# Hybrid decoder layer on one Trainium2 core: heads' keys side by side with zeros for 128-row logits, padded stacks, first transfers on one queue

## The chip, the core and the metric

The kernel runs on one core of one Trainium2 chip. The metric is the device time of one execution in microseconds (us). Times of before are a median of 3 runs; one further execution was profiled. Engines are named as in the profile: PE is the matrix engine, DVE the vector engine, ACT the scalar engine, POOL the GpSimd engine, SP the sync engine (here it only starts transfers). PEld is PE's weight load, which overlaps its matmuls.

## The reference

One decoder layer, with T = 256 positions, width 1024, and four branches of 4 heads by 64, all in fp32:

```python
h = rmsnorm(x, pre_norm_g)
proj = einsum('btd,dc->btc', h, w_in)            # 1024 x 4104
p_gdn, p_hgrn, p_moba, p_diff = split(proj)
y = concat([gdn_branch(p_gdn, ...),              # gated delta rule, chunks of 64
            hgrn2_branch(p_hgrn, ...),           # gated linear recurrence, chunks of 16
            moba_branch(p_moba, slopes_moba),    # one block of 256 keys: causal attention with ALiBi
            diff_branch(p_diff, ...)])           # softmax(q1 k1) - lam * softmax(q2 k2), 32 rows each
y = einsum('btc,cd->btd', y, w_out)              # 1024 x 1024
x = x + rmsnorm(y, post_norm_g)
```

In both attentions the logits of a head are its queries times its keys: 64 deep in MoBA, twice 32 deep in the differential attention. Each branch's output is multiplied by SiLU of its own gate.

## The kernel before

**Arithmetic.** An fp32 product is made of three matmuls. A weight piece (`raw`) is split into a high part in the format fp32r (`whi`, a copy on ACT) and a remainder (`wlo`, a subtraction on DVE); the activations are split likewise into `hT_hi` (ACT) and `hT_lo` (DVE), for 8 slices (k-tiles) of 128 of the 1024 columns. Then hi times hi, hi times lo and lo times hi are summed in PSUM. Small products of the branches (logits, transposes, chunks of the recurrences) are plain fp32.

**Pieces.** `w_in` comes in 32 pieces of two k-tiles each (512 or 520 KB), `w_out` in 8 of 512 KB. In the order of the program: `gkq` (GDN's keys and queries), `gv` (its values and gates), `mqk` (MoBA), `dqk` (differential), `mvz`, `hqf` and `hiz` (HGRN), `dvz`, then `w_out`. Four pieces make one projection. `raw` is a ring of 6 buffers, `whi` and `wlo` rings of 4. So a split waits until PE has used the piece four before it, and a transfer until DVE has split the piece six before it.

**The start.** The transposed `x` (`pxt`) comes in 5 transfers: `h_kd` holds the constants and k-tile 0 (145.5 KB), the four `prob` tiles hold k-tile 1 (128 KB) and k-tiles 2 and 3, 4 and 5, 6 and 7 (256 KB each). ACT's queue starts all five; SP's queue starts the weights. The first weight piece comes and is split in halves, the others whole. PE is kept at work by WARM matmuls on zeros until the first operands are there.

**The order.** Each operation is recorded with its engine, a cost and what it depends on (`record`). `plan` then orders every engine's stream by list scheduling: of the operations that are ready in its model, the one with the greatest rank goes next. The rank is the longest chain of costs behind an operation, plus a boost and a lead for its part of the program (`LEAD`; m and d are the logits of MoBA and differential attention, g GDN, h HGRN, M and D the values of the two attentions, o the output projection). `HOLD` is how much rank ACT gives up to stay with its table of functions, `STAY` how much PE gives up to stay in its tile shape; `LAT` and `free` are what the model holds for hand-offs and for the first moment of an engine. `emit` issues all of it from L392, so nearly every row of the profile has that line, and rows are told apart by their tiles. Engines only run their streams in that order and wait at each instruction for its operands.

**The logits.** PE works in tile shapes (rows by columns): 128 by 128 in the projections, 64 by 128 in MoBA's logits, 64 by 64 in GDN, 96 by 128 in the differential logits. MoBA's keys are `m_k` on the tile `kf`: head 2hp + hh stands in rows 64hh to 64hh + 63 of column block hp. `moba` loops over query blocks j (0 and 1) and over hh, and `softmax_unit` does two 64-row matmuls each, one for each hp. Then come two maxima on DVE (`prob` and `mx`), two exponentials on ACT, a reciprocal on DVE (`m_sum`), two scalings on ACT, and transposes on PE (`probs_t`). In the differential branch `d_st` holds 96 rows of stacked parts (32 by 3), which POOL's transfers (`move`) fill from `d_ks` and `qk4k`.

**HGRN's values.** `vexp` holds each chunk's values in its own 32 rows and zeros elsewhere; it is zeroed once at the start (128 by 2048) and filled late by 4 transfers of SP.

Of the kernel before, what the change touches and what calls it, by code (L numbers as in the profile page):

```python
# [29 lines left out]
D = 1024  # L30
T = 256
# [55 lines left out]
WARM = 18  # L87
# [10 lines left out]
class Core:  # L98
# [5 lines left out]
    HOLD = 71859  # L104
    SWITCH, KEEP, STAY = 95, 1e9, 10357
    LEAD = {'h': 9467, 'g': 7491, 'o': -78342, 'M': -634, 'x': 25587, 'm': 2702, 'd': 2886, 'D': 6239}
    WINDOW = 4096 / 1.2
    LAT = {"PE": 200, "DVE": 170, "ACT": 170, "POOL": 170, "SP": 1900}
# [186 lines left out]
    def plan(self, noise=None):  # L295
# [3 lines left out]
        lat = lambda p, o: 0 if p.eng == o.eng and p.eng == "PE" else (90 if p.eng == o.eng and p.fn != "dma_start" else p.lat)  # L299
# [13 lines left out]
        free = dict(dict.fromkeys(self.engines, 0.0), SP=500.0)  # L313
# [92 lines left out]
def _build(c, x, pxt, w_in, w_out, cst, prow, out, dbg):  # L406
# [14 lines left out]
    XPARTS = [(1, 2), (2, 4), (4, 6), (6, 8)]  # L421
# [20 lines left out]
    def piece(key, k):  # L442

        if (key, k) not in HI:
            t = c.tmp("raw", [128, 2, 520], bufs=6)
            first = not HI
# [3 lines left out]
            c.boost = turn(k) - 0.05 * BOOST if lead < 8 else turn(8) if lead < 10 else 0.0  # L450
            if first:
                c.dma(t[:, 0, :w], part[:, 0])
                c.boost = turn(1) - 0.05 * BOOST
                c.dma(t[:, 1, :w], part[:, 1])
            else:
                c.dma(t[:, :, :w], part)
            split([(key, k), (key, k + 1)], t[:, :, :w], first)
        return HI[key, k], LO[key, k]

    def split(keys, raw, apart=False):  # L460

        w = raw.shape[2]
        c.boost = BOOST
        hi = c.tmp("whi", [128, 2, 520], bufs=4, dt=FR)[:, :, :w]
        lo = c.tmp("wlo", [128, 2, 520], bufs=4, dt=FR)[:, :, :w]
        for i in ([slice(0, 1), slice(1, 2)] if apart else [slice(0, 2)]):
            if apart and i.start == 0:
# [380 lines left out]
    def hgrn_v(pi):  # L848

        vh = c.tile("h_v", [128, 2, 256])  # L850
        for j in range(2):
            act(vh[:, j, :], pi[j], AF.Copy, scale=rs[:, j:j + 1])
        for q in range(4):
            r = slice(32 * q, 32 * q + 32)
            c.dma(vexp[r, :, q, :], vh[r, :, :])
        return vh

    def hgrn(pq, pf, vh):
# [42 lines left out]
        for j in range(2):  # L901
            pu = c.bank("gB" if j == 0 else "gA")
            n = 4 - j
            for hp in range(2):
                for hh in range(2):
                    h = 2 * hp + hh
                    mm(pu[64 * hh:64 * hh + 64, hp * 256:hp * 256 + n * 64], kdh[:, j, h * 64:(h + 1) * 64],
                       vexp[:, j, 0:n, h * 64:(h + 1) * 64])
# [49 lines left out]
    def softmax_unit(bank, lhs, rhs, slope, j, dst, sums):  # L958


        nk = 128 * (j + 1)
        pb = c.bank(bank)
        for hp in range(2):
            mm(pb[:, hp * nk:(hp + 1) * nk], lhs[:, hp, j * 128:(j + 1) * 128], rhs[:, hp, 0:nk])
        mx = c.tmp("mx", [128, 4], bufs=4)
        for hp in range(2):
            c.vec("tensor_tensor_reduce", dst[:, hp, 0:nk],
                  dict(in0=pb[:, hp * nk:(hp + 1) * nk], in1=cs[:, K_DIST + 256 - nk:K_DIST + 256]), scale=1.0,
                  scalar=-3.0e38, op0=OP.add, op1=OP.max, accum_out=mx[:, hp:hp + 1])
        k0 = slope(0)[0]  # L970
        c.tt(mx[:, 2:4], mx[:, 0:2], cs[:, k0:k0 + 3:2], OP.mult)
        for hp in range(2):
            act(dst[:, hp, 0:nk], dst[:, hp, 0:nk], AF.Exp, scale=slope(hp)[1], bias=mx[:, 2 + hp:3 + hp],
                accum_out=sums[:, hp:hp + 1])

    def probs_t(pt, hh, j, P, bank):
        pb = c.bank(bank)
        i = 0
        for hp in range(2):
            for b in range(j + 1):  # L980
                tr(pb[:, i * 128:(i + 1) * 128], P[:, hp, b * 128:(b + 1) * 128], ident)
                i += 1
        o = 2 * j
        act(pt[:, hh, o:o + i].rearrange("p a b -> p (a b)"), pb[:, 0:i * 128], AF.Copy)
# [59 lines left out]
    def diff(pq, pk):  # L1044
# [20 lines left out]
        for hh in range(2):  # L1065
            P = []
            for w in range(2):
# [5 lines left out]
                for j in range(2):  # L1073
                    P.append(c.tmp("prob", [128, 2, 256], bufs=4))
                    softmax_unit("wB", st[0:96, 0], st[0:96, 1],
                                 lambda hp: (K_SL + 4 + 2 * hp + hh, 2.0 ** -(2 * (2 * hp + hh) + 1)), j, P[-1],
                                 sums[:, w, hh, j])
            for j in range(2):
# [7 lines left out]
                probs_t(pt, hh, j, P[j], "wA")  # L1086
# [155 lines left out]
```

## Time and profile before

| | us |
|---|---|
| median of 3 runs | 174.97 (173.48 to 176.22) |
| profiled execution | 175.41 |
| its span in the trace | 173.7 |
| PE busy | 160.8 (93%) |
| PEld busy | 140.1 (81%) |
| DVE busy | 132.9 (77%) |
| ACT busy | 106.8 (61%) |
| POOL busy | 15.7 (9%) |

The span begins and ends inside the execution: 1.7 us of the profiled time lie outside it. A row of a timeline has the start, the length, the engine and the operation with its output and inputs; in brackets stands how long the engine had been idle just before and what ended that. Matmuls are pipelined, so a row's length is longer than its step: the step is read from one start to the next. On PE one fp32 matmul leaves two records, an fp32r matmul one.

### The profile page before, as it was taken

Reading aid. Unit: us, or ns where it says so; the run is one execution under the profiler, and the core shown is the slowest. Engines: PE = TensorE matmul, PEld = TensorE weight load, DVE = VectorE, ACT = ScalarE, POOL = GpSimd, SP = SyncE. Lnnn points to the kernel's source line nnn. Section 1 sums busy time; section 2 is a strip of 40 time slices with the busy share of each in tenths; the row PEclk is TensorE's granted clock in tenths of the full one; section 3 lists DMA queues with packets and bytes.
Section 4 is the critical chain, followed back from the end, with each engine's and each line's share of the span. In section 5 each row is a group of like instructions: output and inputs, shape, how many; then the busy total and the mean of one; then the engine's idle time right before and its main releaser. Section 6 shows DMA issues by size and latency. Waiting matters only on the chain.

```text
span 173.7 us, 3605 instructions
## 1 busy us (share of the span) xinstructions
PE 160.8 (93%) x1358; PEld 140.1 (81%) x1358; DVE 132.9 (77%) x354; ACT 106.8 (61%) x211; POOL 15.7 (9%) x35
## 2 busy tenths in 40 slices
PE   7759999999999999699999997999999999999960
PEld 4559999899997999698788994776877768987850
DVE  0777599695798999994656996976889668759472
ACT  2684757999634264424598928898699631366440
POOL 8000000000000000265007500000000000000000
PEclk9858999999999999999999999999999999999997
DMA  5999897266194037335004899457706100000033
GB/s 164 339 415 418 338 367 261 55 202 199 53 312 157 0 116 235 138 76 110 0 4 91 218 296 398 149 180 246 248 0 189 56 0 0 4 0 0 0 121 121
DMA packets 14176, 27.24 MB, mean 157 GB/s; under 512 B 1360, under 2 KB 2640, under 8 KB 14160
## 3 DMA queue, kind: packets, MB, share of 16 engines
q1 hardware_dynamic: 12288, 24.39, 40.8%
q0 software_dynamic: 1152, 1.57, 4.4%
q10 hardware_dynamic: 720, 1.07, 2.0%
q8 instruction: 10, 0.16, 0.4%
q14 instruction: 6, 0.05, 0.1%
HBM read 24.14 MB, written 1.05 MB: 145 GB/s over the span
## 4 chain that ended last, share of the span: by engine, by line
PE 74%; DVE 12%; DMA 7%; ACT 2%; issue 1%; ACTq 1%; DVEq 0%
PE pj L392 49%; PE gA L392 7%; PE gB L392 7%; PE wB L392 6%; PE wA L392 6%; DVE wlo L392 5%; DMA prob<-in_pxt_dram 4%; DMA raw<-in_w_in_dram 3%; DVE g_nb L392 2%; ACT whi L392 1%; DVE g_vb L392 1%; ACTq L392 1%; DVE g_y L392 1%; DVE b4k L392 1%; DVE lf L392 1%
## 5 line engine op out<-in xcount | busy, mean ns | idle before, releaser
L392 DVE TENSOR_TENSOR wlo<-raw,whi 128x1024 fp32r<-128x1024 f32 (+2 forms) x41 | 48.1, 1197 | 11.1 <-ACT whi L392 6.4
L392 ACT ACTIVATE whi<-raw 128x1024 fp32r<-128x1024 f32 (+2 forms) x40 | 41.4, 1047 | 19.1 <-PE pj L392 12.0
L392 PE MATMUL pj<-hT_hi,whi 128*128 128x256 f32 x144 | 38.8, 293 | 4.1 <-ACT whi L392 1.9
L392 PE MATMUL pj<-hT_lo,whi 128*128 128x256 f32 x144 | 38.1, 290 | 0.0
L392 PEld LDWEIGHTS pj<-hT_hi,whi 128*128 128x128 f32 x144 | 28.1, 196 | 6.0 <-ACT whi L392 3.8
L392 PE MATMUL pj<-hT_hi,wlo 128*128 128x256 f32 x144 | 28.9, 292 | 0.2 <-DVE wlo L392 0.2
L392 PEld LDWEIGHTS pj<-hT_lo,whi 128*128 128x128 f32 x144 | 28.1, 197 | 0.1
L392 PE MATMUL pj<-whi,hT_lo 128*128 128x512 f32 (+2 forms) x80 | 26.7, 348 | 0.0
L392 PEld LDWEIGHTS pj<-hT_hi,wlo 128*128 128x128 f32 x144 | 22.2, 194 | 0.9 <-DVE wlo L392 0.6
L392 PE MATMUL pj<-wlo,hT_hi 128*128 128x512 f32 (+2 forms) x64 | 21.3, 348 | 0.7 <-DVE wlo L392 0.7
L392 PE MATMUL pj<-whi,hT_hi 128*128 128x512 f32 (+2 forms) x64 | 21.4, 342 | 0.5 <-DVE gz_moba L392 0.5
L392 PEld LDWEIGHTS pj<-whi,hT_lo 128*128 128x128 f32 x80 | 15.0, 188 | 1.7
L392 PEld LDWEIGHTS pj<-whi,hT_hi 128*128 128x128 f32 x64 | 12.0, 189 | 2.1 <-DVE gz_moba L392 0.9
L390 ACT ACT_TABLE_LOAD x9 | 11.5, 1283 | 3.4 <-issue 3.2
L392 PEld LDWEIGHTS pj<-wlo,hT_hi 128*128 128x128 f32 x64 | 11.6, 188 | 2.3 <-DVE wlo L392 1.1
L392 ACT ACTIVATE prob<-prob,mx 128x128 f32<-128x128 f32 (+1 forms) x24 | 10.7, 448 | 3.4 <-DVE mx L392 3.3
L392 DVE CUSTOM_DVE_ANT_0 prob<-wB,cs 128x128 f32<-128x128 f32 (+1 forms) x24 | 7.8, 356 | 6.4 <-PE wB L392 6.4
L392 POOL DMA_DIRECT2D d_st<-d_ks x12 | 6.1, 506 | 68.2 <-ACT d_ks L392 68.2
L392 PE MATMUL pj<-whi,d_st 128*128 128x512 f32 (+1 forms) x32 | 10.1, 390 | 0.0
L392 POOL DMA_DIRECT2D d_st<-qk4k x12 | 5.9, 492 | 13.5 <-PE wB L392 11.8
L392 PEld LDWEIGHTS pj<-whi,d_st 128*128 128x128 f32 x32 | 5.4, 189 | 1.1 <-DVE d_st L392 0.2
L392 ACT ACTIVATE t2k<-pj 128x512 f32<-128x512 f32 (+1 forms) x4 | 2.2, 544 | 5.3 <-PE pj L392 5.3
(269 smaller groups left out, 287.4 us busy)
## 6 DMA issues: line engine op xcount, KB each, us to landing
raw<-in_w_in_dram SPq DMA_DIRECT2D x27, 512.0 KB, 5.9
raw<-in_w_out_dram SPq DMA_DIRECT2D x8, 512.0 KB, 4.5
raw<-in_w_in_dram SPq DMA_DIRECT2D x4, 520.0 KB, 8.2
xs<-in_x_dram SPq DMA_DIRECT2D x2, 512.0 KB, 8.5
prob<-in_pxt_dram ACTq DMA_DIRECT2D x3, 256.0 KB, 6.8
d_st<-d_ks POOLq DMA_DIRECT2D x12, 64.0 KB, 2.0
d_st<-qk4k POOLq DMA_DIRECT2D x12, 64.0 KB, 2.0
raw<-in_w_in_dram SPq DMA_DIRECT2D x2, 256.0 KB, 3.7
```

The lines of the kernel that those rows point to most:

```text
L390: nc.scalar.add_instruction(mybir.InstLoadActFuncSet(name=nc.get_next_instruction_name(), act_func_set_id=cur, ins=[], outs=[]))
L392: getattr(self.engines[o.eng], o.fn)(*o.args, **o.kw)
```

## The change

- **MoBA's keys.** `m_k` is now [128, 2, 2, 256]: for each hp and hh a block of 256 columns that holds the keys of head 2hp + hh in their 64 rows and zeros in the other 64. One 128-row matmul gives the logits of both heads of a pair side by side (256 columns for j = 0, 512 for j = 1), where two 64-row ones were. The loop runs over hp where it ran over hh, and the maxima, exponentials and transposes follow. `m_k` stands on the first of two halves of what was `vexp`.
- **Padding.** Rows 96 to 127 of both `d_st` buffers are zeroed once by POOL, and the differential logits read 128 rows.
- **Zeros for HGRN.** `vexp` is split into two tiles. `spread` zeroes both on POOL behind MoBA's logits, and the values come in 8 transfers of 32 KB, not 4 of 64 KB.
- **The start.** The transfers of k-tiles 1 to 7 of `x` go from ACT's queue to SP's, where they stand between the weight pieces in the order of k. The second weight piece is loaded and split in halves too. The copy of the constants `pc` gets the lowest rank in place of the common one.
- **Numbers of the planner**: WARM, HOLD, STAY, LEAD, LAT and `free`.

```diff
-WARM = 18
+WARM = 19
-    HOLD = 71859
-    SWITCH, KEEP, STAY = 95, 1e9, 10357
+    HOLD = 34479
+    SWITCH, KEEP, STAY = 95, 1e9, 8733
...
-    for a, b in XPARTS:
+    for a, b in ((1, 2), (2, 4), (4, 6), (6, 8)):
         c.boost = turn(a)
         c.dma(xr[a // 2][:, a % 2:a % 2 + b - a],
-              pxt[:, P_END + a * T:P_END + b * T].rearrange("p (k t) -> p k t", t=T), "ACT")
+              pxt[:, P_END + a * T:P_END + b * T].rearrange("p (k t) -> p k t", t=T))
...
+            first = lead < 4
             if first:
-                c.dma(t[:, 0, :w], part[:, 0])
-                c.boost = turn(1) - 0.05 * BOOST
-                c.dma(t[:, 1, :w], part[:, 1])
+                for i in range(2):
+                    c.boost = turn(k + i) - 0.05 * BOOST
+                    c.dma(t[:, i, :w], part[:, i])
...
+    spare = [c.tile("vexp", [128, 4, 256], tag=f"vexp_{j}") for j in range(2)]
-    c.memset(vexp, 0.0)
+    c.memset(spare[0], 0.0)
+    for i in range(2):
+        c.memset(c.tile("d_st", [128, 2, 2, 256], tag=f"d_st_{i}")[96:128], 0.0)
...
-            c.dma(vexp[r, :, q, :], vh[r, :, :])
+            for j in range(2):
+                c.dma(spare[j][r, q, :], vh[r, j, :])
...
-        km = c.tile("m_k", [128, 2, 256], tag="kf")
+        km = c.tile("m_k", [128, 2, 2, 256], tag="vexp_0")
-        c.tt(km, two3(pk), rrow2, OP.mult)
+        for hh in range(2):
+            r = slice(64 * hh, 64 * hh + 64)
+            c.tt(km[r, :, hh], two3(pk)[r], rrow2[r], OP.mult)
...
-            for hh in range(2):
-                r = slice(64 * hh, 64 * hh + 64)
+            nk = 128 * (j + 1)
+            for hp in range(2):
                 P = c.tmp("prob", [128, 2, 256], bufs=4)
-                softmax_unit("wB", qm[r], km[r], ...)
+                pb = logits("wB", [(0, qm[:, hp, j * 128:(j + 1) * 128], km[:, hp, :, 0:nk])])
+                softmax_unit(pb, K_SL + 2 * hp, 1, 4 * hp + 2, 2, nk, P, sums[:, j, hp])
...
+        spread()
...
-                    softmax_unit("wB", st[0:96, 0], st[0:96, 1], ...)
+                    pb = logits("wB", [(hp * nk, st[:, 0, hp, j * 128:(j + 1) * 128], st[:, 1, hp, 0:nk])
+                                       for hp in range(2)])
```

The first place where instructions move is SP's queue at the start of the program. `raw` are weight pieces and `prob` the later k-tiles of `x` (a number behind a name is its buffer). Before:

```order
L392 DMA raw_93<-in_w_in_dram 128x512 x2
L392 DMA raw_96<-in_w_in_dram 128x2x512
L392 DMA raw_99<-in_w_in_dram 128x2x512
L392 DMA raw_102<-in_w_in_dram 128x2x512
L392 DMA raw_108<-in_w_in_dram 128x1040
L392 DMA xs<-in_x_dram 128x1024 x2
```

Now:

```order
L392 DMA raw_96<-in_w_in_dram 128x512 x2
L392 DMA prob_68<-in_pxt_dram 128x256
L392 DMA raw_99<-in_w_in_dram 128x512
L392 DMA prob_69<-in_pxt_dram 128x512
L392 DMA raw_99<-in_w_in_dram 128x512
L392 DMA raw_102<-in_w_in_dram 128x2x512
L392 DMA prob_70<-in_pxt_dram 128x512
L392 DMA raw_105<-in_w_in_dram 128x2x512
L392 DMA prob_71<-in_pxt_dram 128x512
L392 DMA raw_111<-in_w_in_dram 128x1040
L392 DMA xs<-in_x_dram 128x1024 x2
```

The four `prob` transfers stood on ACT's queue behind `h_kd`; now each stands ahead of the weight piece that is used after it, and the second piece is in halves.

The second place is DVE's stream from the split of the first `dqk` pieces to GDN's products. `wlo` are splits, `kf` and `vexp_86` hold MoBA's keys, `lf` its queries, `prob` and `mx` (ISA rows) its maxima, names with g_ are GDN's. Before:

```order
L392 TENSOR_TENSOR wlo_104<-raw_102,whi_103 128x2x512
L392 COPY g_gc<-gA_83 128x8
L392 SCALAR_TENSOR_TENSOR g_kd<-g_lk,gA_83 128x8
L392 TENSOR_TENSOR kf<-pj_92,rrow 128x512
L392 SCALAR_TENSOR_TENSOR g_gc<-g_lk,g_gc 128x8
L392 SCALAR_TENSOR_TENSOR g_gc<-g_lq,g_gc 128x8
L392 SCALAR_TENSOR_TENSOR g_b<-g_lk,g_gc 128x8
L392 TENSOR_TENSOR g_gc<-g_gc,g_u 128x8
L392 SCALAR_TENSOR_TENSOR lf<-pj_91,cs,rrow 128x256
L392 COPY g_bh<-g_b 64x2x2 x4
L392 SCALAR_TENSOR_TENSOR lf<-pj_91,cs,rrow 128x256
L392 TENSOR_TENSOR g_kdec<-cs,g_bh 128x512
```

Now, from a little later:

```order
L392 TENSOR_TENSOR g_kdec<-cs,g_bh 128x512
L392 ISA prob_69,mx_152<-wB_150,cs 128x128
L392 ISA mx_152 128x1
L392 TENSOR_TENSOR g_ee<-gA_83,g_kdec 128x512
L392 TENSOR_TENSOR g_ee<-gB_118,g_kdec 128x512
L392 RECIPROCAL m_sum<-m_sum 128x2
L392 ISA prob_70,mx_153<-wB_150,cs 128x256
L392 ISA mx_153 128x1
L392 TENSOR_TENSOR mx_152<-mx_152,cs 128x2
L392 TENSOR_TENSOR g_eb<-qk4k,g_eb 128x512
L392 TENSOR_TENSOR mx_153<-mx_153,cs 128x2
L392 TENSOR_TENSOR g_ee<-gA_83,g_ee 128x256 x2
```

All of MoBA's maxima, which stood behind GDN's products before, now stand among them.

The third place is PE's stream, where MoBA's logits (`wB`) for j = 0 meet projections (`pj`) and GDN (`gA`, `gB`). Before:

```order
L392 MATMUL wA_78<-ident,prob_68 128x128
L392 MATMUL gA_83<-g_xa,g_ee 64x64 x16
L392 MATMUL wB_148<-kf,lf 128x128 x2
L392 MATMUL wA_78<-ident,prob_68 128x128
L392 MATMUL pj_92<-hT_hi,whi_103 128x256
```

Now:

```order
L392 MATMUL gA_83<-g_g,cs 128x8 x2
L392 MATMUL pj_110<-hT_lo,whi_100 128x256
L392 MATMUL pj_110<-hT_hi,wlo_101 128x256
L392 MATMUL pj_110<-hT_hi,whi_100 128x256
L392 MATMUL gA_83<-g_gm,ones 64x8 x2
L392 MATMUL gA_83<-ident,t2k_82 128x128 x2
L392 MATMUL wB_150<-vexp_86,lf 128x256
L392 MATMUL pj_110<-hT_lo,whi_100 128x256
```

A pair of 64-row matmuls (`kf`, between other tile shapes) is one 128-row matmul on `vexp_86`, and it stands among projections of the same shape, at the start of GDN rather than behind it. Over the whole stream PE changes its tile shape 59 times before and 46 times now; ACT loads a table 9 times before and 11 times now.

## Rows read from the trace of the kernel before

**Rows 1.** The page: its first line, the busy times, and the gigabytes a second in 40 equal slices of the span (4.34 us each).

```profile
span 173.7 us, 3605 instructions
PE 160.8 (93%) x1358; PEld 140.1 (81%) x1358; DVE 132.9 (77%) x354; ACT 106.8 (61%) x211; POOL 15.7 (9%) x35
...
GB/s 164 339 415 418 338 367 261 55 202 199 53 312 157 0 116 235 138 76 110 0 4 91 218 296 398 149 180 246 248 0 189 56 0 0 4 0 0 0 121 121
```

**Rows 2.** The chain that ended last, in order of time: start, length, what it was spent on.

```profile
2.21 6.83 DMA prob<-in_pxt_dram
...
10.57 12.05 PE pj L392 x84
...
166.87 1.08 PE gA L392 x9
```

**Rows 3.** The start in four stretches, by windows: stretch, its length, then the busy time and number of instructions of PE, PEld, DVE, ACT and POOL, the granted clock of PE (1.00 is 2.4 GHz, 0.50 is 1.2 GHz), the DMA engines' share and GB/s.

```profile
4.35:7.77 3.42, 2.38 (x13) 1.72 (x13) 2.67 (x7) 1.80 (x5) 0.21 (x1) 1.00 1.00 332
7.77:10.57 2.80, 0.91 (x6) 0.62 (x4) 1.39 (x4) 2.33 (x5) 0.00 (x0) 0.50 1.04 391
10.57:14.59 4.02, 4.02 (x19) 4.02 (x20) 4.02 (x5) 3.15 (x5) 0.00 (x0) 0.50 1.04 421
14.59:22.00 7.41, 7.41 (x64) 7.41 (x64) 4.71 (x8) 4.66 (x7) 0.00 (x0) 1.00 0.95 370
```

**Rows 4.** ACT's timeline at the start: its queue's starts of four transfers (ACTq), then casts of the activations, and of the second weight piece.

```profile
1.23 1.96 ACTq L392 DMA_DIRECT2D prob<-in_pxt_dram  x4
...
5.41 0.51 ACT L392 ACTIVATE hT_hi<-prob,h_kd 128x256 fp32r<-128x256 f32 x1 [0.38 <-DMA prob<-in_pxt_dram]
...
7.67 0.91 ACT L392 ACTIVATE hT_hi<-prob,h_kd 128x256 fp32r<-128x256 f32 x2 [1.23 <-DMA prob<-in_pxt_dram]
9.06 0.51 ACT L392 ACTIVATE hT_hi<-prob,h_kd 128x256 fp32r<-128x256 f32 x1 [0.47 <-DMA prob<-in_pxt_dram]
9.47 1.04 ACT L392 ACTIVATE whi<-raw 128x1024 fp32r<-128x1024 f32 x1
```

**Rows 5.** PE's timeline where the first projection (`gkq`) gives way to the second (`gv`), and two steps of a projection at 47 us.

```profile
22.09 0.41 PE L392 MATMUL pj<-whi,hT_hi 128*128 128x264 f32 x2
...
47.25 0.28 PE L392 MATMUL pj<-hT_hi,whi 128*128 128x256 f32 x1
...
47.97 0.28 PE L392 MATMUL pj<-hT_hi,whi 128*128 128x256 f32 x1
```

**Rows 6.** PE's timeline around two of MoBA's logits groups; 64*128 is the tile shape.

```profile
63.38 0.28 PE L392 MATMUL pj<-hT_hi,whi 128*128 128x256 f32 x1
63.59 0.71 PE L392 MATMUL wB<-kf,lf 64*128 64x128 f32 x4
64.23 0.38 PE L392 MATMUL pj<-whi,hT_lo 128*128 128x256 f32 x1
...
82.48 1.13 PE L392 MATMUL wB<-kf,lf 64*128 64x256 f32 x4
```

**Rows 7.** PE's timeline: the four longest idle times between 25 and 165 us.

```profile
53.91 0.33 PE L392 MATMUL gA<-qk4k 64*64 64x128 f32 x2 [0.39 <-ACT g_eb L392]
...
71.94 0.35 PE L392 MATMUL pj<-hT_hi,whi 128*128 128x256 f32 x1 [1.44 <-DVE g_nb L392]
...
107.22 0.50 PE L392 MATMUL pj<-wlo,hT_hi 128*128 128x512 f32 x1 [0.74 <-DVE wlo L392]
...
108.67 0.50 PE L392 MATMUL pj<-whi,hT_hi 128*128 128x512 f32 x1 [0.48 <-DVE gz_moba L392]
```

**Rows 8.** DVE's timeline from the split of the first `dqk` piece to the last of GDN's first products, and PE's row that needs the latter's bank.

```profile
44.63 1.23 DVE L392 TENSOR_TENSOR wlo<-raw,whi 128x1024 fp32r<-128x1024 f32 x1 [3.13 <-PE pj L392]
...
56.72 0.41 DVE L392 TENSOR_TENSOR g_ee<-gB,g_ee 128x256 f32<-128x256 f32 x1
...
57.40 0.60 PE L392 MATMUL gB<-ident,v_diff 128*128 128x128 f32 x4
```

**Rows 9.** Groups of instructions by form: count, busy time in us, mean ns of one, idle time before them and what ended it. The two kinds of `prob` on DVE serve MoBA (4 each) and the differential branch (8 each).

```profile
L392 DVE CUSTOM_DVE_ANT_0 prob<-wB,cs 128x256 f32<-128x256 f32 x12 | 4.6, 422 | 1.9 <-PE wB L392 1.8
L392 DVE CUSTOM_DVE_ANT_0 prob<-wB,cs 128x128 f32<-128x128 f32 x12 | 3.2, 290 | 4.6 <-PE wB L392 4.6
L392 DVE TENSOR_TENSOR mx<-mx,cs 128x2 f32<-128x2 f32 x12 | 1.9, 159 | 0.2
L392 DVE TENSOR_TENSOR kf<-pj,rrow 128x512 f32<-128x512 f32 x2 | 1.4, 684 | 0.0
L392 DVE TENSOR_TENSOR wlo<-raw,whi 128x512 fp32r<-128x512 f32 x2 | 1.4, 684 | 0.0
L392 ACT ACTIVATE prob<-prob,mx 128x256 f32<-128x256 f32 x12 | 6.0, 500 | 0.1
L392 ACT ACTIVATE prob<-prob,mx 128x128 f32<-128x128 f32 x12 | 4.7, 395 | 3.3 <-DVE mx L392 3.3
L390 ACT ACT_TABLE_LOAD x9 | 11.5, 1283 | 3.4 <-issue 3.2
```

**Rows 10.** Windows of later stretches, with the columns of rows 3.

```profile
70.00:110.00 40.00, 37.34 (x412) 32.14 (x411) 31.25 (x114) 25.37 (x64) 11.81 (x24) 1.00 0.53 151
110.00:168.00 58.00, 57.89 (x426) 46.19 (x424) 44.59 (x103) 35.76 (x74) 0.00 (x0) 1.00 0.25 81
```

**Rows 11.** POOL's timeline at the start: the zeros for `vexp`.

```profile
1.82 1.80 POOL L392 MEMSET vexp<- 128x2048 f32 x1
```

More of the change, by code (lines that the diff above doesn't have):

```diff
@@ L103 @@
     OUT = ("out", "accum_out", "dst")
-    HOLD = 71859
-    SWITCH, KEEP, STAY = 95, 1e9, 10357
-    LEAD = {'h': 9467, 'g': 7491, 'o': -78342, 'M': -634, 'x': 25587, 'm': 2702, 'd': 2886, 'D': 6239}
+    HOLD = 34479
+    SWITCH, KEEP, STAY = 95, 1e9, 8733
+    LEAD = {'h': 7522, 'g': 6523, 'o': -111940, 'M': 5144, 'x': 39478, 'm': 28417, 'd': 3696, 'D': 2624}
     WINDOW = 4096 / 1.2
-    LAT = {"PE": 200, "DVE": 170, "ACT": 170, "POOL": 170, "SP": 1900}
+    LAT = {"PE": 200, "DVE": 170, "ACT": 170, "POOL": 170, "SP": 2600}
     def __init__(self, ctx, tc):
@@ L312, in plan @@
         ready = {e: [] for e in self.engines}
-        free = dict(dict.fromkeys(self.engines, 0.0), SP=500.0)
+        free = dict(PE=1150.0, DVE=880.0, ACT=800.0, POOL=0.0, SP=800.0)
         events = [(0.0, 0, i) for i, o in enumerate(ops) if not o.left]
@@ L449, in piece, with split @@
             lead = sum(1 for q in HI if q[0] != "o")
-            c.boost = turn(k) - 0.05 * BOOST if lead < 8 else turn(8) if lead < 10 else 0.0
+            first = lead < 4
             if first:
-                c.dma(t[:, 0, :w], part[:, 0])
-                c.boost = turn(1) - 0.05 * BOOST
-                c.dma(t[:, 1, :w], part[:, 1])
+                for i in range(2):
+                    c.boost = turn(k + i) - 0.05 * BOOST
+                    c.dma(t[:, i, :w], part[:, i])
             else:
+                c.boost = turn(k) - 0.05 * BOOST if lead < 8 else turn(8) if lead < 10 else 0.0
                 c.dma(t[:, :, :w], part)
-            split([(key, k), (key, k + 1)], t[:, :, :w], first)
+            split([(key, k), (key, k + 1)], t[:, :, :w], first, not lead)
         return HI[key, k], LO[key, k]
-    def split(keys, raw, apart=False):
+    def split(keys, raw, apart=False, first=False):
         w = raw.shape[2]
@@ L466, in split @@
         for i in ([slice(0, 1), slice(1, 2)] if apart else [slice(0, 2)]):
-            if apart and i.start == 0:
+            if first and i.start == 0:
                 c.copy(hi[:, i], raw[:, i])
@@ L559, in _build, with spread @@
     sall = c.tile("sall", [128, 8, 2, 64])
-    vexp = c.tile("vexp", [128, 2, 4, 256])
+    spare = [c.tile("vexp", [128, 4, 256], tag=f"vexp_{j}") for j in range(2)]
     ath = c.tile("ath", [128, 2, 4, 128])
-    c.memset(vexp, 0.0)
+    c.memset(spare[0], 0.0)
+    for i in range(2):
+        c.memset(c.tile("d_st", [128, 2, 2, 256], tag=f"d_st_{i}")[96:128], 0.0)
+    def spread():
+        for t in spare:
+            c.memset(t, 0.0)
     c.memset(ath, 0.0)
@@ L907, in hgrn @@
                     mm(pu[64 * hh:64 * hh + 64, hp * 256:hp * 256 + n * 64], kdh[:, j, h * 64:(h + 1) * 64],
[L908 removed]
+                       spare[j][:, 0:n, h * 64:(h + 1) * 64])
             for q in range(n):
@@ L955, in hgrn, with logits, softmax_unit, probs_t @@
         finish_y("hgrn", y, "gB")
-    def softmax_unit(bank, lhs, rhs, slope, j, dst, sums):
-        nk = 128 * (j + 1)
+    def logits(bank, parts):
         pb = c.bank(bank)
-        for hp in range(2):
-            mm(pb[:, hp * nk:(hp + 1) * nk], lhs[:, hp, j * 128:(j + 1) * 128], rhs[:, hp, 0:nk])
+        for o, lhs, rhs in parts:
+            mm(pb[:, o:o + c.size(rhs)], lhs, rhs)
+        return pb
+    def softmax_unit(pb, k0, step, h0, dh, nk, dst, sums):
         mx = c.tmp("mx", [128, 4], bufs=4)
[L966 to L976, printed above, removed]
+        for i in range(2):
+            c.vec("tensor_tensor_reduce", dst[:, i, 0:nk],
+                  dict(in0=pb[:, i * nk:(i + 1) * nk], in1=cs[:, K_DIST + 256 - nk:K_DIST + 256]), scale=1.0,
+                  scalar=-3.0e38, op0=OP.add, op1=OP.max, accum_out=mx[:, i:i + 1])
+        c.tt(mx[:, 2:4], mx[:, 0:2], cs[:, k0:k0 + step + 1:step], OP.mult)
+        for i in range(2):
+            act(dst[:, i, 0:nk], dst[:, i, 0:nk], AF.Exp, scale=2.0 ** -(h0 + i * dh), bias=mx[:, 2 + i:3 + i],
+                accum_out=sums[:, i:i + 1])
+    def probs_t(dst, j, P, bank):
         pb = c.bank(bank)
         i = 0
-        for hp in range(2):
+        for m in range(2):
             for b in range(j + 1):
-                tr(pb[:, i * 128:(i + 1) * 128], P[:, hp, b * 128:(b + 1) * 128], ident)
+                tr(pb[:, i * 128:(i + 1) * 128], P[:, m, b * 128:(b + 1) * 128], ident)
                 i += 1
-        o = 2 * j
-        act(pt[:, hh, o:o + i].rearrange("p a b -> p (a b)"), pb[:, 0:i * 128], AF.Copy)
+        act(dst, pb[:, 0:i * 128].rearrange("p (m b q) -> p m b q", m=2, q=128), AF.Copy)
     def attend(pt, vm, bank):
```

27 lines of the change are left out of this document (12 added, 15 removed).

## The prediction

> **What bounds the kernel now.** I read the page first. PE is busy 160.8 of 173.7 us, DVE 132.9 and ACT 106.8 [rows 1]: PE is the bound, and DVE is far enough up to become one locally. Then the chain that ended last: it is a transfer of `x` up to 9.04 us, then PE in long pieces to 167.95 us, with a tail of some 6 us that no part of the change touches [rows 2]. So only three things pay: PE starting earlier, PE needing less time, and PE waiting less.
>
> The start is the one long loss. In the windows PE does 13 instructions up to 7.77 us, only 6 in the next 2.80 us, then runs without a break, but at the 1.2 GHz level for 4.02 us (19 instructions) before the clock is back at 2.4 GHz [rows 3]. The fall comes with the pause: clock 1.00 in the stretch before it and 0.50 in the one with PE busy 0.91 of 2.80 us. ACT shows what was late: three casts of the activations end idle times of 0.38, 1.23 and 0.47 us on the transfers of `x`, and the whole second weight piece is only cast from 9.47 [rows 4]. Meanwhile the DMA engines moved 332 to 421 GB/s [rows 3]: they were full, with pieces that were not needed yet. GDN's first projection gives way to the second at 22.09 [rows 5].
>
> Behind that PE is nearly closed. Its four longest waits are 0.39, 1.44, 0.74 and 0.48 us, three of them on DVE [rows 7]; from 110 to 168 us it is busy 57.89 of 58.00 [rows 10].
>
> **The change, part by part.**
>
> *The start.* All weights and `x` up to k-tile 7 are 3.09 MB (145.5 + 128 + 3 x 256 KB and four pieces of 512). The slices moved 0.71 + 1.47 MB by 8.7 us and then 415 GB/s [rows 1], so in strict order everything is there at about 10.9 us, and the half pieces early: the 1.3 MB up to k-tile 3's `x` by about 6.1 us by the same slices. SP takes on four more starts and one for the half; four took ACT 1.96 us [rows 4], 0.49 each, so the tenth transfer is started by about 5.3 us, well ahead of its turn. ACT is rid of them, but its first cast waits for `h_kd` anyway. From k-tile 2 on, ACT needs a cast of `x` (0.51, [rows 4]) and half a weight piece's cast (about 0.5) per k-tile, DVE the same and a half split of 0.68 [rows 9], against 12 steps of PE. A step at 2.4 GHz is 7.41/64 = 0.116 to 0.72/6 = 0.12 [rows 3, 5]; I take 0.118, so PE needs 1.42 per k-tile and is the slowest. I leave the first 13 steps where they are and let the second piece start at 7.3 (`x` at about 6.1 to 6.7, cast and split behind it). The first projection has 96 steps; 83 x 0.118 = 9.8, so it ends at 17.1 in place of 22.09: **-5.0**. It could be 0.9 better, since the first 13 need 1.53 and were busy 2.38 [rows 3], and 2.0 worse if the clock falls all the same (half of the 4.02 us).
>
> *Tile shapes.* The 64-row logits come 0.21 after a step of 0.118, and the next projection 0.64 after them for four records [rows 6]. A record of 128 columns is worth (1.13 - 0.71)/4 = 0.105 [rows 6], so going in costs 0.09 and coming out up to 0.22. There are 13 changes of shape fewer. I take 0.095 each, near the first row: **-1.2**; the ends are 0, if the cost lies beside other work, and 2.0 at the mean of the two.
>
> *The matmuls themselves.* MoBA's logits go from 4 matmuls of 128 and 4 of 256 columns to 2 of 256 and 2 of 512: the same columns. In before's pairs both matmuls stand in the same 64 rows, and four records of 128 columns took 0.71 [rows 6], so no time was shared that could now be lost. The padding to 128 rows changes no column. Both: 0. *A rule against it:* the Trainium skill, "TensorEngine Tiling (Array Packing)", section "Key Properties", says that different tiles can load and multiply in parallel, so two 64-row products could share the array where one padded product fills it. By that the old logits would have taken half. The rows show full length.
>
> *Waits that go.* The late wait on `wlo` (0.74) follows from weights refilled late, that on `gz_moba` (0.48) from DVE being late there; with DVE relieved behind 70 us, where it had 31.25 of 40 us [rows 10] and all MoBA's maxima, and the first wait (0.39, on ACT) in a stretch that is reordered, I count all three as gone: **-1.6** (0 to -3.1). The 1.44 on `g_nb` I keep, since GDN's solve remains.
>
> *Waits that come.* The new order puts MoBA's maxima among GDN's products on DVE. I follow both engines to one point: PE's transposes of `v_diff`, which need the bank that DVE's last `g_ee` product reads. Before, DVE went from 44.63 to 57.13 and PE stood there at 57.40 [rows 8]. After, PE would be there at 57.40 - 5.0 - 0.4 (the wait that goes) - 0.9 (282 projection steps ahead of that point, 290 before) + 2.9 (all MoBA's logits: twice about 0.45 and twice about 0.9, and two transposes) = 54.0. DVE starts at 44.63 - 5.0 = 39.6, since its first split waited for PE, needs its old 12.5 and 3.9 more: four `prob` each of 0.38 and 0.27, four `mx` of 0.16, and the keys in two halves of 0.68 for one whole [rows 9]. That is 56.0, and 56.3 with the 0.27 between the two rows of before: 2.3 late. Besides, DVE may wait for PE's logits: 6.5 us over 24 rows before, 0.27 each [rows 9], for eight of them 0 to 2.2; I take 0.9, because GDN's work stands between. Queued behind are the split of the next weight piece and so PE's projections. **+3.2** (2.3 to 4.5).
>
> *Covered, at nothing.* POOL's zeros: `vexp` took 1.80 for 2048 columns [rows 11]; two `d_st` of 1024 and half of `vexp` are less than as much again and end before MoBA needs them; uncovered up to 1. Two more table loads of 1.28 [rows 9]: ACT is busy 25.37 of 40 us and 35.76 of 58 [rows 10]; uncovered 2.6. The 8 transfers of `vexp` stand between `w_out` pieces on SP, where the DMA engines are at a share of 0.25 [rows 10]; four more starts are 2.0 if uncovered. Zeroing by `spread` (about 1.8) lies ahead of POOL's moves for the differential logits, which PE needs tens of us later.
>
> **Sum.** -5.0 - 1.2 - 1.6 + 3.2 = -4.6: a span of 169.1 and, with the 1.7 outside, **170.8 us**. The profiled execution (175.41) is 0.4 above the median, inside the three runs.
>
> **The rivals.**
>
> *DVE keeps pace.* If ACT's and PE's parts of MoBA fall so that DVE never makes PE wait, the 3.2 go: 167.6. For it: DVE idles 8.75 us between 70 and 110 [rows 10]. Against: the count above, which finds it late by durations alone.
>
> *The clock falls again.* If one late operand leaves a pause after the first steps, as in rows 3, the start gains 2.0 less: 172.8. For it: the first piece is still followed by transfers of 3.09 MB in one line. Against: 1.42 of PE per k-tile against about 1.1 on ACT and 1.2 on DVE.
>
> *MoBA's softmax stands in GDN's way.* One unit is a chain over three engines: logits 0.45 (0.9 for j = 1), maxima and `mx` 0.7 (1.0), two exponentials with read-out about 1.2 (1.4), reciprocal 0.16, two scalings 0.8 (1.0), transposes and their copy 0.7 (0.9): 4.0 and 5.3, for four units 18.6 [rows 6, 9]. The streams are fixed, so GDN's products behind a `prob` wait for it. With a third uncovered (6.2 in place of 3.2) it is 173.8, with half 176.9: I put 175.3. For it: ACT waited 3.3 us on `mx`, DVE 4.6 on the logits [rows 9]. Against: four buffers of `prob`. **Slower** from 178.5 on, when 10.9 of the 18.6 stay uncovered; with two thirds (12.4) it is 180.0.
>
> *The old logits shared the array.* By the packing rule the change takes back half of 2.7 us: 172.1. Rows 6 speak against it.
>
> **How the numbers follow.** My forecast 0.46, DVE keeps pace 0.15, the clock falls again 0.15, the softmax in the way 0.14, so far that it is slower 0.07, shared array 0.03. About 2% is what a measurement tells from no change, so faster is below 171.5, slower above 178.5. Of my forecast, whose own range by the bounds is 168.8 to 172.6, some seven tenths is faster; with the first rival and a little of the clock's that is 0.50, to which I add 0.06 for a start better by up to 0.9; slower is 0.07, the rest 0.37. The range runs from 167.0 to 175.5: it leaves out half of the first rival and the upper half of the softmax one.
>
> **What would show it.** First step: windows with PE at clock 1.00 throughout and `gv`'s first row near 17.1; wrong if a window at 0.50 stays. Tile shapes: MoBA's logits without a step over 0.12 beside them. Waits that come: DVE without idle time from 40 to 56 us, and PE's transposes of `v_diff` near 56 with a wait on `g_ee`; wrong if PE waits on ACT's `prob` or not at all. Waits that go: PE full from 100 to 110 us. The whole is wrong if PE's idle time between 40 and 110 us exceeds 7 us.

## The result and the profile after

The changed kernel took 168.40 us (median of 4 runs, 168.21 to 168.66), the kernel before beside it 175.08; the ratio is 0.9649 (0.9582 to 0.9715). The forecast was 170.8 with a range of 167.0 to 175.5: right in sign and range, and 2.4 us too long. The profiled execution took 168.47 us, 1.8 of it outside the span, so the span shows where 7.0 us went.

The page of the changed kernel, to be read against [rows 1]:

```profile
span 166.7 us, 3622 instructions
PE 157.4 (94%) x1351; PEld 138.1 (83%) x1351; DVE 133.0 (80%) x356; ACT 108.3 (65%) x214; POOL 18.8 (11%) x39
```

DVE has as much work as before in a shorter span; PE has 3.4 us less busy time and 3.6 us less idle time. The start by windows, against [rows 3]:

```profile
4.35:7.77 3.42, 3.15 (x18) 2.46 (x16) 2.48 (x8) 2.21 (x5) 2.46 (x4) 1.00 0.99 308
7.77:10.57 2.80, 2.40 (x20) 2.40 (x21) 1.99 (x4) 2.09 (x4) 0.00 (x0) 1.00 1.05 405
10.57:14.59 4.02, 4.02 (x36) 4.02 (x36) 3.73 (x6) 3.68 (x7) 0.00 (x0) 1.00 1.04 414
```

From 4.35 to 14.59 us PE has done 74 instructions where it had done 38, the granted clock stays at its 2.4 GHz level, and the DMA engines move no more than before (308 to 414 GB/s, before 332 to 421): the bytes are the same, their order is not. PE's timeline at the points that answer to [rows 5, 8], and all its waits over 0.2 us from the start's last on, against [rows 7]:

```profile
8.17 0.50 PE L392 MATMUL pj<-hT_hi,whi 128*128 128x256 f32 x2 [0.65 <-ACT hT_hi L392]
...
17.73 0.41 PE L392 MATMUL pj<-whi,hT_hi 128*128 128x264 f32 x2
...
55.58 0.38 PE L392 MATMUL gB<-ident,v_diff 128*128 128x128 f32 x2
...
59.67 0.44 PE L392 MATMUL wA<-ident,prob 128*128 128x128 f32 x2 [0.25 <-ACT prob L392]
...
77.19 1.15 PE L392 MATMUL gA<-g_xa,g_ee 64*64 64x64 f32 x32 [1.03 <-DVE g_xa L392]
```

The second projection begins at 17.73 in place of 22.09. The waits of 0.39, 0.74 and 0.48 us are gone; the 1.44 on DVE's solve has a successor of 1.03, 5 us later. No idle time stands in front of the `v_diff` row at 55.58, where the forecast had PE wait for DVE. From the second projection's first row to `v_diff` PE was idle 0.23 us in all (37.85 less 37.62); windows of the changed kernel, then of the kernel before:

```profile
17.73:55.58 37.85, 37.62 (x313) 34.38 (x312) 34.46 (x97) 29.06 (x63) 0.95 (x1) 1.00 0.64 221
```

```profile
22.09:57.40 35.31, 34.92 (x312) 33.53 (x311) 29.76 (x71) 25.22 (x44) 0.00 (x0) 1.00 0.57 193
```

DVE around the point at which the forecast made it late, and its groups against [rows 9]:

```profile
39.10 4.63 DVE L392 TENSOR_TENSOR wlo<-raw,whi 128x1024 fp32r<-128x1024 f32 x4 [0.61 <-ACT whi L392]
...
54.89 0.42 DVE L392 TENSOR_TENSOR g_ee<-gB,g_ee 128x256 f32<-128x256 f32 x1
```

```profile
L392 DVE CUSTOM_DVE_ANT_0 prob<-wB,cs 128x256 f32<-128x256 f32 x12 | 4.7, 421 | 1.1 <-PE wB L392 1.0
L392 DVE CUSTOM_DVE_ANT_0 prob<-wB,cs 128x128 f32<-128x128 f32 x12 | 3.2, 287 | 0.7 <-PE wB L392 0.5
```

DVE goes from 39.10 to 55.31, and PE's transposes of `v_diff` start 0.27 later without having waited. Its waits for logits fell from 6.5 to 1.8 us over the 24 rows. DVE sets the pace from 46.90 on, and longer than before. In the changed kernel the chain that ended last comes to DVE there and, but for two pieces of 0.95 us without a cause in the profile, stays on DVE up to the wait of 1.03:

```profile
46.90 0.29 DVE prob L392
...
76.43 0.72 DVE g_xa L392
77.19 1.15 PE gA L392 x32
```

In the kernel before it came to DVE at 47.46, was back at PE from 53.91 to 60.50, and left DVE again at 71.94:

```profile
47.46 1.80 DVE wlo L392 x2
...
53.91 1.09 PE gA L392 x16
...
60.50 0.37 DVE g_nb L392 x2
...
71.94 6.96 PE pj L392 x57
```

### The profile page after: what moved, and what is told of

It is laid out like the page before. It is cut to its first block, busy times and chain, and to the rows that moved or that the text cites. A ratio compares the mean times of both kernels' runs of the same rounds, so it can differ in the third digit from the quotient of the medians.

```text
span 166.7 us, 3622 instructions
## 1 busy us (share of the span) xinstructions
PE 157.4 (94%) x1351; PEld 138.1 (83%) x1351; DVE 133.0 (80%) x356; ACT 108.3 (65%) x214; POOL 18.8 (11%) x39
## 4 chain that ended last, share of the span: by engine, by line
PE 60%; DVE 23%; DMA 9%; issue 3%; ACT 2%; SPq 1%; DVEq 0%; ACTq 0%
PE pj L392 39%; DMA raw<-in_w_in_dram 9%; PE gA L392 7%; PE gB L392 6%; PE wB L392 4%; PE wA L392 4%; DVE g_nb L392 4%; DVE wlo L392 3%; DVE g_ee L392 2%; DVE y L392 1%; DVE g_kdec L392 1%; DVE g_y L392 1%; DVE prob L392 1%; ACT whi L392 1%; DVE g_vb L392 1%
## 5 line engine op out<-in xcount | busy, mean ns | idle before, releaser
L392 DVE TENSOR_TENSOR wlo<-raw,whi 128x1024 fp32r<-128x1024 f32 (+2 forms) x42 | 48.3, 1173 | 12.4 <-ACT whi L392 7.6
L392 PE MATMUL pj<-hT_hi,whi 128*128 128x256 f32 x144 | 36.8, 289 | 0.7 <-ACT hT_hi L392 0.7
L392 PE MATMUL pj<-hT_lo,whi 128*128 128x256 f32 x144 | 36.5, 288 | 0.0
L392 PEld LDWEIGHTS pj<-hT_hi,whi 128*128 128x128 f32 x144 | 26.6, 190 | 1.9 <-ACT hT_hi L392 1.4
L392 PEld LDWEIGHTS pj<-hT_lo,whi 128*128 128x128 f32 x144 | 26.3, 188 | 0.3 <-issue 0.2
L392 PE MATMUL pj<-wlo,hT_hi 128*128 128x512 f32 (+2 forms) x64 | 19.9, 353 | 0.2 <-DVE wlo L392 0.2
L392 PEld LDWEIGHTS pj<-wlo,hT_hi 128*128 128x128 f32 x64 | 11.1, 189 | 1.6 <-DVE wlo L392 0.4
L392 PE MATMUL pj<-whi,d_st 128*128 128x512 f32 (+1 forms) x32 | 9.1, 371 | 0.0
L392 POOL MEMSET vexp<- 128x1024 f32 x3 | 2.8, 948 | 46.6 <-PE wB L392 46.6
L392 ACT ACTIVATE g_za<-gA 32x256 f32<-32x256 f32 x2 | 0.8, 376 | 9.9 <-PE gA L392 9.8
```

What stands on the lines that cost most here:

```text
L392: getattr(self.engines[o.eng], o.fn)(*o.args, **o.kw)
```

## The experiments

**The theory** after the result: the start brings its gain by the order of the bytes; behind it the new order of MoBA's softmax costs DVE less, and saves more later, than was forecast; shapes cost about 0.1 us a change. **The rivals**: one part alone brings the gain (the planner's numbers, or the logits); the start's gain is given back; shapes are free or shared. Times below are medians beside the kernel before on the same chip, in brackets the ratio to it with its interval.

**One part alone, and each left out.** The change has three parts: the start, the logits (with padding and zeros), the planner's numbers. The edits are hunks of the diff, for the start for instance

```diff
-              pxt[...].rearrange("p (k t) -> p k t", t=T), "ACT")
+              pxt[...].rearrange("p (k t) -> p k t", t=T))
...
-            first = not HI
+            first = lead < 4
```

The start alone. 

> The kernel before with the start of the change alone (transfers of x on SP's queue in the order of k, second piece in halves, constants' copy last), the old logits and the old planner's numbers. Theory A (the start is worth what it is worth by itself, since PE is the bound behind it): the second projection's first row comes near 17.7 us in place of 22.09, no window at the half clock, and the time falls by 4.4 us to about 170.7. Rival (what the start gains is given back behind it, at DVE or at the refill of weights, unless the order is made anew): the row comes near 17.7, and the time is 173 to 175.

The logits alone. 

> The kernel before with the logits of the change alone (keys side by side with zeros, padded stacks, split vexp), the old start and the old planner's numbers. Theory A (fewer changes of tile shape at 0.1 us each, nothing else): 173.5 to 175, the start's rows as in the kernel before. Rival (the new logits take waits away behind the start by themselves): 172 to 173.

The numbers alone. 

> The kernel before with the planner's numbers of the change alone. Theory A (the numbers fit an order to the code and bring little with the old code): 174 to 177. Rival (the order alone brings the 2.6 us that the changed kernel gains behind the start): 172 to 173.

Start and logits, old numbers. 

> The changed kernel with the old planner's numbers: start and logits of the change. Theory A (the start's 4.4 us stay, and of the 2.6 us behind it only the tile shapes' part does): 169.5 to 171, the second projection's first row near 17.7. Rival (the numbers do nothing): 168.2 to 168.7.

Logits and numbers, old start. 

> The changed kernel with the old start (x on ACT's queue, second piece whole, constants' copy as before), new logits and new planner's numbers. Theory A: it loses what the start is worth, 4.4 us, and ends near 172.8, with a stretch at the half clock behind 7.8 us. Rival (part of the start's gain is lost later anyway): 170 to 171.5.

Start and numbers, old logits. 

> The changed kernel with the old logits (64 and 96 rows, one vexp): new start, new planner's numbers. Theory A (the logits bring some tile shapes and hardly more): 169 to 170. Rival (the logits bring the gain behind the start): 170.5 to 171.5.

| parts in | us | ratio |
|---|---|---|
| start | 172.40 | 0.992 (0.9883 to 0.9957) |
| logits | 176.35 | 1.0147 (1.0073 to 1.022) |
| numbers | 173.02 | 0.9917 (0.9883 to 0.995) |
| start, logits | 171.83 | 0.9864 (0.9814 to 0.9913) |
| logits, numbers | 170.40 | 0.9797 (0.9731 to 0.9863) |
| start, numbers | 170.25 | 0.9791 (0.9748 to 0.9834) |
| all | 168.39 | 0.9663 (0.9614 to 0.9712) |

None of the six came out in the theory's figures. With the old start it was the rival's 170 to 171.5; without the logits it lay between theory and rival; the start alone, the logits alone and the old numbers were longer than the theory said; the numbers alone shorter, at the rival's edge. No single part does it: alone they come to 0.8% less, 1.5% more and 0.8% less, together to 3.4% less. The logits are a loss with the old start and numbers, and worth 1.3% on top of the other two. The theory's 4.4 us for the start were wrong as time: it gives 0.8% alone and 1.3% on top of the rest, 1.4 and 2.3 us. Nor was it given back behind, as the rival had it. Both had put the second projection's first row near 17.7; with the start alone it came at 19.16, 2.9 earlier than in the profiled execution of before, and that span is 2.8 shorter (170.9 and 173.7). PE's later waits are 1.9 us in sum, where before had 3.05. What is missing to 17.7 is the pace of PE's first steps. One window, two rows out of it, and the second projection's:

```profile
7.77:10.57 2.80, 2.80 (x15) 2.58 (x15) 2.11 (x4) 2.27 (x5) 0.00 (x0) 1.00 1.04 385
```

```profile
9.14 0.41 PE L392 MATMUL pj<-hT_hi,wlo 128*128 128x256 f32 x1
9.36 0.41 PE L392 MATMUL pj<-hT_hi,whi 128*128 128x256 f32 x1
...
19.16 0.40 PE L392 MATMUL pj<-whi,hT_hi 128*128 128x264 f32 x2
```

PE is never idle in that window and its granted clock reads 1.00, but until 9.6 us most steps are 0.21 to 0.22 us apart, as in the half-clock stretch of before (19 in 4.02 us), and not 0.12. The two other profiled runs with the new start and old numbers show the same up to 10.1 us, with the second projection at 19.65 and 19.67. In the six profiled runs with the new start on SP's queue and the new numbers, MoBA's lead aside, most steps are 0.12 us apart from 7 us on, and the row comes at 17.44 to 18.23. So in the traces 1.4 to 2.2 us are gained only by start and numbers together; which number it is was not tried.

With the old start and all else new, the windows and the second projection's first row show why the start is worth 2.3 and not 4.4:

```profile
4.35:7.77 3.42, 2.62 (x17) 2.00 (x16) 2.83 (x6) 1.70 (x4) 2.56 (x4) 1.00 1.02 333
7.77:10.57 2.80, 0.62 (x6) 0.42 (x5) 1.02 (x4) 2.08 (x4) 0.00 (x0) 1.00 1.02 376
10.57:14.59 4.02, 4.02 (x30) 3.71 (x31) 3.66 (x6) 3.50 (x7) 0.00 (x0) 1.00 1.04 423
```

```profile
20.34 0.41 PE L392 MATMUL pj<-whi,hT_hi 128*128 128x264 f32 x2
```

The pause is there (PE busy 0.62 of 2.80), but the clock stays at its 2.4 GHz level behind it. So 2.6 us of the profile's 4.4 (20.34 to 17.73) are there without any half clock; the half clock of the profiled execution of before makes the rest likely, since 19 steps took it 4.02 us where 0.118 each would be 2.24.

**The queue.** The changed kernel's own order, with the four transfers of `x` issued by ACT again.

```diff
+                for p in self.front:
+                    nc.scalar.dma_start(*p.args)
...
```

> The changed kernel in its own order of instructions on every engine, with only the four transfers of x put back on ACT's queue, all at the front of it; the second piece stays in halves. Theory A (the order in which the bytes come is what counts): x for the late k-tiles again comes ahead of the second piece, whose halves land 1 to 2 us later, PE pauses longer than 0.65 us before the second piece, the second projection's first row comes 1 to 4 us later than 17.7, and the time is 169.5 to 172.5. Rival (the halves alone do it, and the queue is of no account): 168.2 to 168.8.

170.02 us (0.9778, 0.9722 to 0.9834): in the theory's range, but not by its mechanism. ACT's timeline with the transfers on its queue, and then that of the changed kernel:

```profile
1.24 3.38 ACTq L394 DMA_DIRECT2D prob<-in_pxt_dram  x4
4.65 1.28 ACT L390 ACT_TABLE_LOAD   x1 [4.65 <-DMA h_kd<-in_pxt_dram]
5.94 0.51 ACT L397 ACTIVATE hT_hi<-h_kd 128x256 fp32r<-128x256 f32 x1
```

```profile
1.24 1.28 ACT L390 ACT_TABLE_LOAD   x1 [1.24 <-PEq L1250]
4.21 0.51 ACT L392 ACTIVATE hT_hi<-h_kd 128x256 fp32r<-128x256 f32 x1 [1.69 <-DMA h_kd<-in_pxt_dram]
```

The last of the four starts waits for `h_kd` to land (it begins at 4.28), and ACT's table load and first cast stand behind it: the first cast comes at 5.94, not 4.21. The kernel before had four such starts on the same queue without that wait. They took 1.96 us [rows 4], and ACT went on with

```profile
3.22 1.28 ACT L390 ACT_TABLE_LOAD   x1 [3.22 <-issue]
4.52 0.51 ACT L392 ACTIVATE hT_hi<-h_kd 128x256 fp32r<-128x256 f32 x1
```

So the 1.7 us are of this run's own order. Between the kernel before and the changed one ACT's relief is worth 0.3 us at the first cast, close to the nothing of the forecast. Behind the late cast PE's steps are again 0.21 us apart up to 12.4 us, at a granted clock that reads 1.00, and the second projection comes at 20.69, 3.0 later. The longer pause before the second piece that the theory named is not there. So the loss of 1.6 us by the medians (2.0 by the ratios) isolates neither the queue nor the order of the bytes. That the start as a whole is worth 2.3 us rests on the run without it; how much of that the order brings and how much the halves is not shown.

**Tile shapes.** The changed kernel again, for reference on the same chip; then with the differential logits from 96 rows, and with MoBA's logits as 64-row pairs, all three in one order of instructions.

```diff
-pb = logits("wB", [(hp * nk, st[:, 0, hp, ...], st[:, 1, hp, 0:nk]) ...
+pb = logits("wB", [(hp * nk, st[0:96, 0, hp, ...], st[0:96, 1, hp, 0:nk]) ...
```

```diff
+for hh in range(2):
+    r = slice(0, 64)
+    c.nc.tensor.matmul(pb[:, hh * nk:(hh + 1) * nk], lhsT=qm[r, hp, ...], rhs=km[r, hp, hh, 0:nk], ...)
...
```

> The changed kernel once more, on the chip on which the two below are timed: 168.2 to 168.7.

> The changed kernel in its own order of instructions on every engine, with the differential logits read from 96 rows in place of 128: 15 more changes of PE's tile shape, by the neighbours of the 16 matmuls in the order, and the same columns. Theory A (a change of shape costs about 0.1 us on PE, and PE is the bound): 1.0 to 1.5 us slower than the changed kernel. Rival (the changes lie beside other work): within 0.3 us of it.

> The changed kernel in its own order, with each of MoBA's four logits matmuls made as two 64-row matmuls of half the columns; both read the first head's 64 rows, so the second head's logits are left out (two row tiles may not write one bank together). Seven more changes of tile shape, the same columns. Theory A: 0.5 to 0.9 us slower than the changed kernel. Rival (the shapes cost nothing): within 0.3 us. Rival (two 64-row products share the array): faster by up to 1.3 us.

168.39 us (0.9663), 169.18 (0.9704, 0.9647 to 0.9761) and 169.23 (0.9709, 0.9659 to 0.9759). The 64 rows cost 0.84 for 7 changes of shape (0.12 each), and no run of theirs is as short as the longest of the changed kernel. The 96 rows cost 0.8 us by the medians, below the theory's 1.0, but their trace shows no price for the 15 changes. The first of these logits stand at 80.40 us, and at 80.38 in the changed kernel's second trace; the last, and the step behind them, with 96 rows and then with 128:

```profile
105.87 0.40 PE L392 MATMUL wB<-d_st 96*128 96x256 f32 x2
106.11 0.40 PE L392 MATMUL pj<-whi,hT_hi 128*128 128x512 f32 x1
```

```profile
105.82 0.40 PE L392 MATMUL wB<-d_st 128*128 128x256 f32 x2
106.06 0.40 PE L392 MATMUL pj<-whi,hT_hi 128*128 128x512 f32 x1
```

Over all 15 the distance grew by 0.03 us. Two of the six runs, the profiled one among them, took 168.3 to 168.4 us like the changed kernel, the other four 169.1 to 169.5; what made those longer is not shown. One of MoBA's pairs in PE's timeline, with 64 rows and then in the changed kernel:

```profile
45.80 0.71 PE L1054 MATMUL wB<-vexp,lf 64*128 64x128 f32 x4
46.44 0.39 PE L395 MATMUL pj<-hT_lo,whi 128*128 128x256 f32 x1
46.66 0.28 PE L395 MATMUL pj<-hT_hi,wlo 128*128 128x256 f32 x1
```

```profile
46.16 0.70 PE L392 MATMUL wB<-vexp,lf 128*128 128x256 f32 x2
46.51 0.47 PE L392 MATMUL pj<-hT_lo,whi 128*128 128x256 f32 x1
46.81 0.28 PE L392 MATMUL pj<-hT_hi,wlo 128*128 128x256 f32 x1
```

From the logits' start to the second projection step it is 0.86 and 0.65 us: 0.21 for two changes, and the columns cost the same. A step of 0.30 (46.51 to 46.81) stands behind the 128-row pair too, so not all of the price that the forecast read beside the old logits was the shape's. The rival of shared arrays falls: the 64-row form is not faster. The rule that the prediction cites from the Trainium skill ("TensorEngine Tiling (Array Packing)", "Key Properties") is about different tiles; here both products read the same rows, as each pair of the kernel before did. Two products in different rows were not tried.

**MoBA's place.** The changed kernel with the lead of MoBA's logits put back; and the kernel with the old numbers with only that lead made new.

```diff
-    LEAD = {..., 'm': 28417, ...}
+    LEAD = {..., 'm': 2702, ...}
```

> The changed kernel with one number of the planner put back: the lead of MoBA's logits, 28417 in the change, at 2702 as before. PE's logits of MoBA then stand on both sides of its transposes of v_diff and up to 145 rows behind them, where the change has all four ahead. Theory A (MoBA's softmax among GDN's first products is what the new order gains by, since DVE is relieved later): 170 to 172, with PE idle times on DVE between 60 and 110 us. Rival (it is the other numbers): 168.2 to 169. Rival (my predicted wait of 3.2 us was there and is now removed): 165 to 167.

> The changed kernel with the old planner's numbers but for that one, the lead of MoBA's logits, which is 28417 as in the change: all four logits stand ahead of the transposes of v_diff. Theory A: most of the 3.4 us between the run with the old numbers (171.8) and the changed kernel (168.4) come back: 168.5 to 170. Rival (it is the other numbers): 171 to 173.

169.74 us (0.9783, 0.9727 to 0.9839) and 175.80 (1.0135, 1.0075 to 1.0194). The late place costs 1.35 us (2.1 by the ratios), less than the theory's 170 to 172. It has two waits on DVE that the changed kernel has not:

```profile
63.51 0.66 PE L392 MATMUL gB<-ident,v_diff 128*128 128x128 f32 x4 [0.58 <-DVE g_ee L392]
71.56 0.70 PE L392 MATMUL wB<-vexp,lf 128*128 128x256 f32 x2 [0.79 <-DVE mx L392]
```

Their sum is 1.37, but the changed kernel's two, 0.25 and 1.03, are gone here, so PE waits hardly longer behind the start. The span is 1.4 longer: 0.5 of it is there when the second projection begins (18.23 and 17.73), and 0.9 is PE's busy time (158.3 and 157.4 in the pages; 50 changes of tile shape and 46). That waits on DVE are what the late place costs is not shown. The converse fell: with the old numbers the early place makes the kernel 4 us slower than the late one (175.80 and 171.83), against theory and rival. PE's timeline, ACT's, and windows of that run:

```profile
132.49 0.97 PE L392 MATMUL pj<-whi,y_gdn 128*128 128x512 f32 x3 [2.50 <-ACT y_gdn L392]
```

```profile
126.44 1.28 ACT L390 ACT_TABLE_LOAD   x1
127.74 0.63 ACT L392 ACTIVATE m_pt<-m_pt 128x512 f32<-128x512 f32 x1
128.27 2.94 ACT L392 ACTIVATE whi<-raw 128x1024 fp32r<-128x1024 f32 x3
...
131.77 0.67 ACT L392 ACTIVATE y_gdn<-gB,pc 128x512 fp32r<-128x512 f32 x1
```

```profile
128.00:132.50 4.50, 2.00 (x11) 1.41 (x9) 4.50 (x7) 4.50 (x8) 0.00 (x0) 1.00 0.39 130
132.50:142.00 9.50, 9.50 (x66) 8.33 (x66) 6.51 (x19) 5.34 (x8) 0.00 (x0) 0.82 0.15 50
```

The cast of GDN's result stands in ACT's fixed order behind a table load and three casts of `w_out` pieces; PE waits 2.50 us, and then the granted clock is 0.82 on average for 9.5 us: 36% of them at the 1.2 GHz level, by estimate 1.7 us lost. The run with the logits alone waits at the same place, which is enough for its loss of 2.1:

```profile
134.24 1.65 PE L392 MATMUL pj<-whi,y_gdn 128*128 128x512 f32 x3 [2.48 <-ACT y_gdn L392]
```

Which of the other numbers keeps the changed kernel from this was not tried.

## Why the prediction was right, point by point

The sum was -4.6 on the span and came out at -7.0. Its own two points, the second projection's start and PE's `v_diff` row, split it:

- **The start**, forecast -5.0: 22.09 to 17.73, **-4.4**. The pause shrank but did not vanish (0.65 us before 8.17), and the clock stayed up. As a mechanism it was right, but the 4.4 us are not the start's alone: with the new start and the old numbers the row came at 19.16 to 19.67, since PE's first steps were 0.21 us apart. In time the start is worth 2.3 us on top of the rest, since the old start with the new numbers made its pause without the half clock that the profiled execution of before shows.
- **Waits that come**, forecast +3.2: this step failed in its mechanism. Its own sign of being wrong was a PE that does not wait at all, and at `v_diff` PE did not wait; from the second projection on it had been idle **0.23 us**. The sum had DVE 2.3 late there, and both sides of it were off. DVE's 16.4 us of work were right (39.10 to 55.31 is 16.2). But its first split came at 39.10, not at 44.63 - 5.0 = 39.6: in [rows 8] it had waited for PE's release, after the change it waited 0.61 us for ACT's cast, so it was not tied to the start's gain. So DVE was done at 55.31, not at 56.0. And PE came at 55.58, not at 54.0: 0.6 by its smaller gain at the start, 0.7 because its own work from there took 37.6 us and not 36.9, 0.2 by idle time. The 0.9 for waits on logits did not come either. So at this point the rival that DVE keeps pace (167.6) came true. DVE's lateness shows only at 77.19, as the 1.03 us that follow the 1.44 which the forecast kept.
- **Tile shapes and waits that go**, forecast -1.2 and -1.6: 0.4 of the waits lies ahead of `v_diff`. Behind it the span shrank from 116.3 (173.7 - 57.40) to 111.1, by 5.2, of which 2.7 is PE's work that moved ahead (37.62 less 34.92). **-2.5** is left, where 2.4 was forecast. The three waits went as said. The shapes were oversized: of the 59 changes before, 9 were between 96 and 128 rows, which cost nothing in the trace above, and all 9 are gone. Without them it is 50 and 46, by estimate 0.4 us at the 0.1 of the 64 rows. What brought the remaining 0.9 is not shown.
- **Covered, at nothing**: ACT's two further table loads, POOL's zeros and the transfers of `vexp` left no wait on PE.

In sum: -4.4 to the second projection, +2.5 from there to `v_diff` (37.85 in place of 35.31), -5.2 behind it: -7.0, since the terms are rounded. The sum is 2.4 off mainly by the 3.2 of a wait that was not there, less the 0.6 that the start fell short. That 168.40 us still lies in the range is in part luck: two terms erred in opposite directions. The narrower range of 168.8 to 172.6 did not hold it, and is not what the terms' own bounds add up to (166.7 to 176.9). The rivals: the clock's recorded level did not fall again; of MoBA's softmax PE saw one wait, 0.25 us at 59.67, and not 6; the array had not been shared.

## What to carry to other kernels

When several engines run fixed streams, price a late engine from the event that releases it, not from where it stood before, and count the waiting engine's own work up to the same point; here both were off and a wait of 3.2 us came out at none. A planner's numbers belong to the code they were fitted to; here each part gave under 1% or a loss alone, and 3.4% together, so parts of such a change can't be judged one by one. Issuing the first transfers in the order of use, with the second piece in halves, brought 2.3 us here. Read the pace of an engine's first steps from one start to the next, not from the granted clock alone.

## What was not expected of the hardware

A granted clock of 1.00 did not mean that PE kept its pace. In four profiled runs (the start alone, the old numbers, those with MoBA's early lead, and `x` on ACT's queue) PE's first steps were 0.21 us apart, as at the 1.2 GHz level, in windows that read 1.00. In these four PE had stood idle 0.73 to 1.75 us just ahead of its first step. That alone does not decide it: before and with the logits alone it stood idle 0.82 and 1.75 us there, and still had steps of 0.12 at 7.4 us. The cause is not shown.

The clock's recorded fall at the start of the kernel before is probably not in each of its runs. Of 41 runs beside these experiments, 9 had a mean granted clock of 0.973 to 0.977 and a median of 175.0 us, 27 had 0.991 or more and 173.6 us, five lay between. The profiled execution of before, with the fall, has 0.974; where the others' clock fell was not recorded. The kernel with the old start and the rest new made nearly the same pause at full clock. So about 1.4 us of the time before goes with that level, and a profile that caught one kind of run made the start look dearer than it mostly is. The six runs of the changed kernel beside the tile-shape runs all lie within 168.0 to 168.8.
